# One operand group of the up-projection prepared two steps earlier, and four groups of finished outputs formed six steps later

## Chip, cores and metric

One core of a Trainium2 chip runs the whole kernel in one launch. The metric is the device time in microseconds (us), as the median over runs; before the change it is 2288.43 us over 3 runs (2288.39 to 2288.69). All matmuls are on TensorE (PE); VectorE (DVE) and ScalarE (ACT) prepare operands and drain results; SyncE (SP) issues nearly all the DMAs, in program order; GpSimd (POOL) does small copies.

## What is computed

One decoder block over 2048 positions of 1024 channels, in float32. What matters here is the chain of four large products and the norms between them:

```
h = rms_norm(x, norm1_g)
z = einsum('bsd,de->bse', h, w_in)            # in-projection
...                                           # convolutions, RG-LRU scan, gates -> y_mix
x = x + einsum('bse,ed->bsd', y_mix, w_out)   # out-projection
h = rms_norm(x, norm2_g)
u = causal_dwconv(einsum('bsd,df->bsf', h, w_up), ffn_conv_w)   # up-projection
gate, up = split(u, 2)
x = x + einsum('bsf,fd->bsd', gelu(gate) * up, w_down)          # down-projection
return rms_norm(x, final_g)
```

## The kernel before

The sequence is cut into two halves of 1024 positions (`T`), and the phases run one after the other: in-projection and mixers of half 0, out-projection of half 0, in-projection and mixers of half 1, out-projection of half 1 (the "second out-projection"), up-projection of half 0, down-projection of half 0, up-projection of half 1, down-projection of half 1 (the "last phase").

Each float32 operand of a product is split into a high part (ACT, `Copy` to a rounded form) and a low part (DVE, the difference; `split`, L196 and L197), and each product is three matmuls: high by high, high by low, low by high. The out-, up- and down-projections are done in a form of Strassen's method with seven block products in place of eight, so their operands are sums and differences of blocks.

**The sweeps.** An out- or down-projection (`sweeps`, L726 for its matmuls, L739 for its loads) makes seven sweeps over the inner dimension, one for each block product. A sweep of the out-projection has three steps (21 in all, numbered 0 to 20), one of the down-projection six (42, numbered 0 to 41). A step loads one page of weights (`wrw`) and one of the other operand (`wrf`) into four raw tiles (two steps' worth), splits both (`wh`, `wl`, `fh`, `fl`, from a pool `w` of ten pages) and runs 24 matmuls. After a sweep DVE adds the four results into the residual pages (`xr` or `x2r`, L762). At the end of every step `beside(step)` is called, which may put other work there.

**The work beside.** In the second out-projection it is `h_prep(0, k)` (L537 to L559): the preparation of operand group k of the up-projection of half 0. There are four groups; k = 0 is made in the mixers of half 1, k = 1, 2, 3 in this phase. Each loads two pages of the stored residual (`ha`, `hb`, L541, by SP), scales both (L542), forms four sums (`hc`, `hq`, L546 to L549) and splits four operands (`hhB`/`hlB` twice, `hhT`/`hlT`, `ht`): 2 DMAs, 10 DVE instructions, 4 ACT instructions. `ha` and `hb` come from a pool of two pages (tag `a`), so the loads of group k wait until group k-1 is split; the seven result pages come from the pool `act` of 28 pages.

In the last phase it is `down1_beside` (L912 on): the outputs of half 0. They wait only for the last norm, which is worked out early in the up-projection before. Four times, two pages of 512 KB are loaded (`fx`, L917), scaled (L906) and stored four steps later.

**What sets the order.** PE, SP and POOL take their instructions in the order of the program. For DVE and ACT a planner orders the instructions at compile time, by the program's order moved forward by stated priorities: splits of weights by 90 instructions (`HW`), drains of PSUM by 120 (`HP`), the adds after a sweep by 30 (`HE`). `h_prep` and `down1_beside` have none. The engines then run the order they were given. A stored page is sent some steps after it is made (`defer`, `tick`, L193).

Of the kernel before, what the change touches and what calls it, by code (L numbers as in the profile page):

```python
# [15 lines left out]
KC = D // P  # L16
# [52 lines left out]
def block_kernel(  # L69
# [52 lines left out]
    def act(name):  # L122
        return page(name, "act", 28)
# [19 lines left out]
    def flat(t):  # L143
        return t.rearrange("p a b -> p (a b)")
# [39 lines left out]
    def defer(n, dst, src):  # L184
        waiting.append([n, dst, src])
# [77 lines left out]
    def inv_rms(acc, name, parts=None):  # L263
        n = acc.shape[-1]
        terms = parts or mean_split(acc, name)
        pss = [pst(f"ms_{name}_{t}") for t in range(0, n, NB)]
        for i, x in enumerate(terms):
            for b, p in enumerate(pss):
                w, v = (ones_r, r32(x[:, blk(b)])) if i < 2 else (ones, x[:, blk(b)])
                nc.tensor.matmul(p, w, v, start=i == 0, stop=i == len(terms) - 1)  # L270
        with tc.high_priority(offset=HP):
            y = flat(tmp(f"ry_{name}"))[:, :n]
            for b, p in enumerate(pss):
                nc.scalar.activation(y[:, blk(b)], p, AF.Abs_reciprocal_sqrt, bias=eps)
                nc.vector.scalar_tensor_tensor(acc[:, blk(b)], p, EPS, y[:, blk(b)], ALU.add, ALU.mult)
            nc.vector.scalar_tensor_tensor(acc, acc, -0.5, y, ALU.mult, ALU.mult)
            nc.vector.scalar_tensor_tensor(acc, acc, 1.5, y, ALU.add, ALU.mult)
        return acc
# [258 lines left out]
    def h_prep(half, k, rs):  # L537
        a = big(f"ha{half}_{k}", 0)[:, :T]
        b = big(f"hb{half}_{k}", 0)[:, :T]
        for t, kk in ((a, k), (b, k + 4)):  # L540
            nc.sync.dma_start(t, x2_d[half][kk // 2][kk % 2])  # L541
            nc.vector.scalar_tensor_tensor(t, t, col(O_G2 + kk), rs, ALU.mult, ALU.mult)  # L542
        c = flat(tmp(f"hc{half}_{k}"))
        q = flat(tmp(f"hq{half}_{k}"))[:, :NB]
        t0, t1 = blk(0), blk(1)
        nc.vector.tensor_tensor(c[:, t0], a[:, t0], a[:, t1], ALU.subtract)  # L546
        nc.vector.scalar_tensor_tensor(c[:, t1], c[:, t0], -1.0, b[:, t1], ALU.mult, ALU.subtract)
        nc.vector.tensor_tensor(a[:, t1], b[:, t1], a[:, t1], ALU.subtract)
        nc.vector.scalar_tensor_tensor(q, c[:, t1], -1.0, b[:, t0], ALU.mult, ALU.subtract)  # L549
        out = {}  # L550
        for t, names in ((a, ("B11", "T3")), (b, ("B21", "B22")), (c, ("T1", "T2"))):
            hi, lo = act(f"hh{names[0]}{half}_{k}"), act(f"hl{names[0]}{half}_{k}")
            split(flat(hi), flat(lo), t)
            for i, n in enumerate(names):
                out[n] = (hi[:, i, :], lo[:, i, :])
        t4 = act(f"ht{half}_{k}")
        split(t4[:, 0, :], t4[:, 1, :], q)
        out["T4"] = (t4[:, 0, :], t4[:, 1, :])
        return out  # L559
# [243 lines left out]
    def store_done(dst, acc, name):  # L803
        def done(key, m, r):
            if m % 2 == 0:
                return
            mh, t = PLACE[key]
            store_pair(dst[2 * mh + m // 2], t, r, 2 if key == "21" else 4)
            add_squares(acc, t, 0 if key in ("11", "22") and m == 1 else 1, r, f"{name}{key}{m}")

        return done
# [43 lines left out]
    def h_beside(half, at):  # L855
        def beside(s):
            if s in at:
                hs[half].append(h_prep(half, len(hs[half]), rs2[half][0]))

        return beside  # L860

    def res_alloc(key, n):
# [7 lines left out]
        "o",  # L870
        x_residual(1, res_alloc),
        store_done(x2_d[1], ss2[1], "b1"),
        h_beside(0, (3, 8, 14)),
    )

    up_phase(0, hs[0], late_mean(ss2[1], "b1", rs2[1], 1))
# [28 lines left out]
    def scaled(ap, m, rs):  # L905
        nc.vector.scalar_tensor_tensor(ap, ap, col(O_GF + m), rs, ALU.mult, ALU.mult)  # L906
# [3 lines left out]
    terms = []  # L910

    def down1_beside(s):  # L912
        if s >= 4 and s % 4 == 0 and s // 4 <= KC // 2:
            i = s // 4 - 1
            for m in range(2):
                t = act(f"fx{i}_{m}")
                nc.sync.dma_start(flat(t), x3_d[i][m])  # L917
                scaled(flat(t), 2 * i + m, rs3[0])
                defer(4, yT[2 * i + m, :, 0:T], flat(t))
        if s == 6 * (NI // 2) + 1:  # L920
            finish_block(1, inv_rms(accl[1], "l1"))

    def finish_block(t, rs):
        for key in ("12", "22") if t else ("11", "21"):
            mh = PLACE[key][0]
            for p, r in enumerate(kept[key]):
                for m in range(2):
                    c = 4 * mh + 2 * p + m
                    scaled(r[:, m, :], c, rs)
                    defer(4, yT[c, :, T + t * NB : T + (t + 1) * NB], r[:, m, :])  # L930

    def down1_done(key, m, r):
# [3 lines left out]
        with tc.high_priority(offset=HP if key == "21" else 0):  # L936
# [6 lines left out]
            if key == "21" and m == 2:  # L943
                terms.extend(mean_split(accl[0], "l0"))

    sweeps(1, down_w, f_d[1], NI, "d", down_residual(1, lambda key, n: act(n)), down1_done, down1_beside, tail=4)
    finish_block(0, inv_rms(accl[0], "l0", terms))
    while waiting:
# [84 lines left out]
```

## Time and profile before

| | |
|---|---|
| median of 3 runs | 2288.43 us (2288.39 to 2288.69) |
| profiled execution, its own time | 2288.58 us |
| its span, first to last instruction | 2286.8 us |
| mean granted TensorE clock | 0.997 |
| PE busy | 2267.2 us (99%) |
| DVE busy | 1722.8 us (75%) |
| ACT busy | 1132.9 us (50%) |
| second out-projection, first matmul to first matmul of the next phase | 780.56 to 896.92 us |
| last phase, start on the chain | 2041.34 us |

The span is what the trace covers; the execution's own time is 1.8 us longer, for what lies before the first and behind the last instruction. A matmul of 512 columns shows a duration of 389 ns, but they are pipelined: in a full stretch 72 of them take 16.32 us, one each 226.7 ns. A row of the timeline gives start, duration, engine, line, operation, output and inputs, count, and in brackets how long the engine was idle before it and which instruction ended that.

### The profile page before, as it was taken

What the parts mean: (1) busy time and instruction counts of PE and PEld (TensorE: products, weight loads), DVE (VectorE), ACT (ScalarE), POOL (GpSimd) and SP (SyncE); (2) the same over time, 40 slices, a digit from 0 to 9 for tenths busy, and PEclk for the clock granted to TensorE, in tenths of its full rate; (3) what the DMA queues carried; (4) which work ended last, traced back from release to release, by engine and by line L of the source; (5) the groups of instructions that cost most, each with busy time, mean ns of one, the idle gap of its engine ahead of it and who ended that gap; (6) DMA issues with size and microseconds to landing.
All of it is one profiled execution on the core that took longest, in us unless ns stands there. A gap on an engine that the chain in (4) does not pass through costs nothing.

```text
span 2286.8 us, 26184 instructions
## 1 busy us (share of the span) xinstructions
PE 2267.2 (99%) x9984; PEld 1874.0 (82%) x9984; DVE 1722.8 (75%) x1909; ACT 1132.9 (50%) x1242; POOL 154.2 (7%) x232
## 2 busy tenths in 40 slices
PE   9999999999999999999999999999999999999997
PEld 7888888888888878888888888888888888888885
DVE  7665668857667798888888887587888888876556
ACT  6564635554547255544444444354544444443343
POOL 0011000011000000111111100000100000000000
PEclk9999999999999999999999999999999999999999
DMA  6454248777655576223232357676223232359764
GB/s 260 122 134 118 70 161 280 259 203 219 167 149 144 180 268 216 87 97 116 92 117 91 118 187 268 217 242 210 71 97 115 92 115 92 116 184 318 262 189 174
DMA packets 145728, 378.30 MB, mean 165 GB/s; under 512 B 13953, under 2 KB 17153, under 8 KB 145025
## 3 DMA queue, kind: packets, MB, share of 16 engines
q1 hardware_dynamic: 135808, 357.74, 45.3%
q0 software_dynamic: 9792, 18.88, 5.2%
q8 instruction: 78, 1.28, 0.2%
q14 instruction: 50, 0.40, 0.1%
HBM read 289.53 MB, written 124.78 MB: 181 GB/s over the span
## 4 chain that ended last, share of the span: by engine, by line
PE 98%; DVE 1%; issue 0%; DMA 0%; ACT 0%; SPq 0%; DVEq 0%
PE zin_b L236 27%; PE zx L606 23%; PE zc L606 11%; PE dx L726 11%; PE dy L726 9%; PE za L606 6%; PE ox L726 6%; PE oy L726 4%; PE zi_b L236 1%; PE zr_b L236 1%; DVE x2r L906 0%; DMA x<-in_xT 0%; DVE wl_d L197 0%; DVE fl_o L197 0%; PE ms_a L270 0%
## 5 line engine op out<-in xcount | busy, mean ns | idle before, releaser
L236 PE MATMUL zin_b<-xh,wh_in 128*128 128x512 f32 x896 | 276.8, 390 | 2.7 <-ACT xh L409 2.7
L236 PE MATMUL zin_b<-xl,wh_in 128*128 128x512 f32 x896 | 276.6, 390 | 0.3 <-DVE xl L410 0.3
L236 PE MATMUL zin_b<-xh,wl_in 128*128 128x512 f32 x896 | 276.3, 390 | 0.0
L236 PEld LDWEIGHTS zin_b<-xh,wh_in 128*128 128x128 f32 x896 | 168.5, 188 | 38.3 <-ACT xh L409 3.3
L236 PEld LDWEIGHTS zin_b<-xl,wh_in 128*128 128x128 f32 x896 | 168.2, 188 | 36.4 <-DVE xl L410 1.8
L236 PEld LDWEIGHTS zin_b<-xh,wl_in 128*128 128x128 f32 x896 | 168.4, 188 | 35.0
L197 DVE TENSOR_TENSOR fl_d<-wrf_d,fh_d 128x1024 fp32r<-128x1024 f32 x84 | 102.8, 1224 | 121.8 <-ACT fh_d L196 119.4
L196 ACT ACTIVATE fh_d<-wrf_d 128x1024 fp32r<-128x1024 f32 x84 | 89.1, 1061 | 209.1 <-PE dy L726 86.4
L197 DVE TENSOR_TENSOR wla_up<-wra_up,wha_up 128x1024 fp32r<-128x1024 f32 x48 | 58.8, 1226 | 140.5 <-ACT wha_up L196 140.5
L726 PE MATMUL dx<-fl_d,wh_d 128*128 128x512 f32 x384 | 149.5, 389 | 0.8 <-DVE fl_d L197 0.8
L726 PE MATMUL dx<-fh_d,wh_d 128*128 128x512 f32 x384 | 149.4, 389 | 0.0
L726 PE MATMUL dx<-fh_d,wl_d 128*128 128x512 f32 x384 | 149.4, 389 | 0.0
L606 PE MATMUL zc<-hhB,whd_up 128*128 128x512 f32 x384 | 126.0, 389 | 0.0
L299 DVE SCALAR_TENSOR_TENSOR cu<-un,prm,cu 128x1024 f32<-128x1024 f32 x96 | 122.6, 1277 | 4.4 <-ACT cu L295 4.3
L299 DVE SCALAR_TENSOR_TENSOR cg<-ug,prm,cg 128x1024 f32<-128x1024 f32 x96 | 122.8, 1280 | 0.4
L196 ACT ACTIVATE wh_in<-wr_in 128x1024 fp32r<-128x1024 f32 (+1 forms) x62 | 59.8, 972 | 122.2 <-PE zin_b L236 93.4
L617 ACT ACTIVATE ug<-zx 128x512 f32<-128x512 f32 x96 | 57.6, 600 | 125.9 <-PE zx L606 125.9
L606 PE MATMUL zx<-ht,whc_up 128*128 128x512 f32 x384 | 118.2, 389 | 0.0
L197 DVE TENSOR_TENSOR wl_d<-wrw_d,wh_d 128x1024 fp32r<-128x1024 f32 x84 | 102.4, 1220 | 12.8 <-ACT wh_d L196 11.5
L726 PE MATMUL dy<-fh_d,wh_d 128*128 128x512 f32 x288 | 112.0, 389 | 0.0
L726 PE MATMUL dy<-fl_d,wh_d 128*128 128x512 f32 x288 | 112.0, 389 | 0.0
L726 PE MATMUL dy<-fh_d,wl_d 128*128 128x512 f32 x288 | 112.0, 389 | 0.0
(261 smaller groups left out, 5552.5 us busy)
## 6 DMA issues: line engine op xcount, KB each, us to landing
wr_in<-in_w_in SPq DMA_DIRECT2D x54, 512.0 KB, 6.7
wra_up<-in_w_up SPq DMA_DIRECT2D x48, 512.0 KB, 4.7
wrb_up<-in_w_up SPq DMA_DIRECT2D x48, 512.0 KB, 5.3
f_d_T<-cg SPq DMA_DIRECT2D x96, 256.0 KB, 2.5
wrw_d<-sd_d_S SPq DMA_DIRECT2D x48, 512.0 KB, 4.5
wrf_d<-f_d_T SPq DMA_DIRECT2D x48, 512.0 KB, 3.9
f_d_B<-cu SPq DMA_DIRECT2D x72, 256.0 KB, 2.4
wrw_d<-in_w_down SPq DMA_DIRECT2D x36, 512.0 KB, 4.7
```

Source lines behind the costliest of these rows:

```text
L196: nc.scalar.activation(r32(hi), src, AF.Copy)
L197: nc.vector.tensor_tensor(r32(lo), src, hi, ALU.subtract)
L236: nc.tensor.matmul(ps[t], r32(a), r32(b[:, blk(t)]), start=(first and i == 0), stop=(last and i == 2))
L299: nc.vector.scalar_tensor_tensor(dst, src[:, k : k + T], col(o_w + k), dst, ALU.mult, ALU.add)
L606: nc.tensor.matmul(ps, r32(p[:, s]), r32(self.hs[k][x][o]), start=f and i == 0, stop=l and i == 2, skip_group_check=True,)
L617: nc.scalar.activation(dst, self.x, AF.Copy)
L726: nc.tensor.matmul(ps[m], r32(p), r32(x[:, k, :]), start=first and i == 0 and n == 0, stop=(last or not on_x) and i == ni - 1 and n == 2, ...
```

## The change

`h_beside(0, ...)` is called for steps 1, 8 and 14 of the second out-projection in place of 3, 8 and 14: `h_prep(0, 1)` stands at the end of step 1, in front of step 2's loads. In the last phase the four groups of outputs of half 0 are loaded and scaled in steps 10, 14, 18 and 22 in place of 4, 8, 12 and 16; the groups and their order stay the same, and each is stored four steps later as before.

```diff
         "o",
         x_residual(1, res_alloc),
         store_done(x2_d[1], ss2[1], "b1"),
-        h_beside(0, (3, 8, 14)),
+        h_beside(0, (1, 8, 14)),
     )
...
     def down1_beside(s):
-        if s >= 4 and s % 4 == 0 and s // 4 <= KC // 2:
-            i = s // 4 - 1
+        if 10 <= s <= 22 and s % 4 == 2:
+            i = s // 4 - 2
             for m in range(2):
                 t = act(f"fx{i}_{m}")
                 nc.sync.dma_start(flat(t), x3_d[i][m])
```

## Rows read from the trace of the kernel before

**Rows 1.** The page: busy time, share and count of each engine, and the shares of the chain of work that ended last.

```profile
PE 2267.2 (99%) x9984; PEld 1874.0 (82%) x9984; DVE 1722.8 (75%) x1909; ACT 1132.9 (50%) x1242; POOL 154.2 (7%) x232
...
PE 98%; DVE 1%; issue 0%; DMA 0%; ACT 0%; SPq 0%; DVEq 0%
```

**Rows 2.** The waits of PE over the whole span: who waited for whom, us in total, how often, the longest.

```profile
PE oy L726 <- DVE fl_o L197: 1.5, 2, 0.9
...
PE dx L726 <- DVE fl_d L197: 0.8, 1, 0.8
```

**Rows 3.** Busy time of each engine in the first and second sweep of the second out-projection: the window, its length, then busy us and count for PE, PEld, DVE, ACT and POOL, the granted clock, the DMA share and GB/s.

```profile
780.56:796.88 16.32, 16.32 (x73) 13.51 (x72) 13.33 (x15) 4.86 (x6) 0.00 (x0) 1.00 0.55 194
796.88:815.32 18.44, 16.91 (x74) 13.36 (x72) 17.91 (x20) 9.37 (x10) 0.00 (x0) 1.00 0.61 186
```

**Rows 4.** Timeline of PE in that second sweep: the first two matmuls of its second step, and the first two of its third.

```profile
802.32 0.39 PE L726 MATMUL oy<-fh_o,wh_o 128*128 128x512 f32 x1
803.61 0.50 PE L726 MATMUL oy<-fl_o,wh_o 128*128 128x512 f32 x1 [0.90 <-DVE fl_o L197]
...
808.96 0.39 PE L726 MATMUL oy<-fh_o,wh_o 128*128 128x512 f32 x1
809.97 0.50 PE L726 MATMUL oy<-fl_o,wh_o 128*128 128x512 f32 x1 [0.63 <-DVE fl_o L197]
```

**Rows 5.** Timeline of DVE in the same sweep: instructions of `h_prep(0, 1)` (`ha`, `hlB`, `ht`) among the splits of the steps (`wl_o`, `fl_o`).

```profile
797.01 1.28 DVE L542 SCALAR_TENSOR_TENSOR ha<-ha,prm,ss_b 128x1024 f32<-128x1024 f32 x1
...
800.60 1.22 DVE L197 TENSOR_TENSOR wl_o<-wrw_o,wh_o 128x1024 fp32r<-128x1024 f32 x1
...
802.34 1.22 DVE L197 TENSOR_TENSOR fl_o<-wrf_o,fh_o 128x1024 fp32r<-128x1024 f32 x1
...
807.56 1.22 DVE L197 TENSOR_TENSOR hlB<-hb,hhB 128x1024 fp32r<-128x1024 f32 x1
808.70 1.22 DVE L197 TENSOR_TENSOR fl_o<-wrf_o,fh_o 128x1024 fp32r<-128x1024 f32 x1
...
813.24 0.69 DVE L197 TENSOR_TENSOR ht<-hq,ht 128x512 fp32r<-128x512 f32 x1
```

**Rows 6.** Timeline of ACT: the split of step 2's weights, and later two splits, one of `h_prep(0, 1)` and one of a step's weights.

```profile
780.31 1.06 ACT L196 ACTIVATE wh_o<-wrw_o 128x1024 fp32r<-128x1024 f32 x1 [5.91 <-PE zin_b L236]
...
804.19 1.06 ACT L196 ACTIVATE hhB<-ha 128x1024 fp32r<-128x1024 f32 x1 [6.28 <-DVE ha L548]
805.16 1.04 ACT L196 ACTIVATE wh_o<-wrw_o 128x1024 fp32r<-128x1024 f32 x1
```

**Rows 7.** Timeline of SP's queue: the residual page of step 1, the second operand of step 2, the residual page of step 2, the weights of step 3, the first load of `h_prep(0, 1)`, and the weights of step 5.

```profile
756.33 0.40 SPq L527 DMA_DIRECT2D xr<-in_xT  x1
...
757.38 0.37 SPq L739 DMA_DIRECT2D wrf_o<-y_d_B  x1
770.78 0.38 SPq L527 DMA_DIRECT2D xr<-in_xT  x1
771.25 0.42 SPq L739 DMA_DIRECT2D wrw_o<-so_d_S  x1
...
773.59 0.57 SPq L541 DMA_DIRECT2D ha<-x_d  x1
...
790.96 0.32 SPq L739 DMA_DIRECT2D wrw_o<-so_d_S  x1
```

**Rows 8.** Timeline of DVE before that: the last reads of `ha` and `hb` of group 0, the instructions behind its idle stretches, and the second operand's low part of steps 2 (788.58) and 3 (792.56).

```profile
758.94 1.23 DVE L197 TENSOR_TENSOR hlB<-ha,hhB 128x1024 fp32r<-128x1024 f32 x1 [0.53 <-ACT hhB L196]
760.09 1.22 DVE L197 TENSOR_TENSOR hlB<-hb,hhB 128x1024 fp32r<-128x1024 f32 x1
...
769.66 1.29 DVE L379 TENSOR_TENSOR pr<-zin_b,ss_a 128x512 f32<-128x512 f32 x2 [4.28 <-PE zin_b L236]
...
772.00 1.22 DVE L387 TENSOR_TENSOR pr<-pr,cc 128x1024 f32<-128x1024 f32 x1
780.54 1.29 DVE L379 TENSOR_TENSOR sb<-zin_b,ss_a 128x512 f32<-128x512 f32 x2 [7.32 <-PE zin_b L236]
...
788.58 1.22 DVE L197 TENSOR_TENSOR fl_o<-wrf_o,fh_o 128x1024 fp32r<-128x1024 f32 x1
...
792.56 1.23 DVE L197 TENSOR_TENSOR fl_o<-wrf_o,fh_o 128x1024 fp32r<-128x1024 f32 x1 [1.62 <-ACT fh_o L196]
```

**Rows 9.** The waits of SP's queue over the whole span, the row of the residual loads.

```profile
SPq L527 <- PE zin_b L236: 12.9, 1, 12.9
```

**Rows 10.** DMA issues by line: count, KB each, median us from issue to landing.

```profile
wrw_o<-in_w_out SPq DMA_DIRECT2D x18, 512.0 KB, 5.7
...
ha<-x_d SPq DMA_DIRECT2D x8, 512.0 KB, 5.5
hb<-x_d SPq DMA_DIRECT2D x8, 512.0 KB, 6.5
```

**Rows 11.** The windows of the first, second and fourth sweep of the last phase, columns as in the third group.

```profile
2041.34:2073.98 32.64, 32.64 (x145) 27.03 (x145) 24.61 (x24) 12.57 (x13) 0.00 (x0) 1.00 0.82 290
2073.98:2106.62 32.64, 32.64 (x145) 27.03 (x145) 20.79 (x20) 12.35 (x13) 0.00 (x0) 1.00 0.97 336
...
2139.26:2171.90 32.64, 32.64 (x145) 27.03 (x145) 16.90 (x17) 13.12 (x15) 0.00 (x0) 1.00 0.70 230
```

**Rows 12.** Timeline of DVE in the last phase: one scaling of outputs of half 0 (two instructions).

```profile
2103.22 2.48 DVE L906 SCALAR_TENSOR_TENSOR fx<-fx,prm,ss_c 128x1024 f32<-128x1024 f32 x2
```

## The prediction

> **What bounds the kernel now.** I read the shares first: PE is busy 99% of the span and the chain that ended last is PE for 98% of it [rows 1]. So a change can win only where PE stands still, and lose only where it makes PE stand still. Next the waits of PE: two of them, 1.5 us together, are in a `y` sweep of an out-projection and wait for `fl_o`, the low part that DVE makes; one of 0.8 us is in a `dx` sweep [rows 2]. Then the windows by sweep: the first sweep of the second out-projection takes 16.32 us, which is 72 matmuls of 226.7 ns back to back; the second takes 18.44 us, 2.12 us more, with DVE busy 17.91 of them [rows 3]. The timeline of PE places it: in step 4 the second matmul starts 1.29 us after the first in place of 0.23 us, in step 5 it starts 1.01 us after [rows 4]. That is 1.06 and 0.78 us, together 1.84; the other 0.28 us is the pace of the few matmuls that follow a stop. The order of DVE says why: the `h_prep(0, 1)` instructions stand between the splits of steps 4 and 5 from 797.01 to 813.93 us, and `fl_o` of step 4 starts only at 802.34, that of step 5 at 808.70, behind `hlB` [rows 5].
>
> **Part 1, the operand group two steps sooner.** It moves 2 loads on SP, 10 instructions on DVE and 4 on ACT; none is added or removed, and POOL's queue has none of it. On DVE: two scalings of 1.28 us, four sums of 512 columns of 0.69 us each (the form of `ht`), three low parts of 1.22 us and `ht` of 0.69 us [rows 5]: 2.56 + 2.76 + 3.66 + 0.69 = 9.7 us. On ACT: three high parts of 1.06 us [rows 6] and half a one, about 3.7 us.
>
> *When the loads can go.* They stand behind step 1's residual load, issued at 756.33 [rows 7]. `ha` needs the page whose last reader, `hlB` of group 0, ends at 760.17, `hb` the one that ends at 761.31 [rows 8]; 5.5 and 6.5 us to landing [rows 10] give about 766 and 768 us. Before they were issued at 773.59 [rows 7].
>
> *What is queued behind them on SP.* Step 2's loads, the second issued at 757.38 [rows 7], move to about 762; with 5.7 us to landing [rows 10] they are there at 768 and are first read at 780.31 [rows 6]: 12 us of cover, cost nothing. Then step 2's residual load, which already waits 12.9 us for a page that PE's last in-projection frees [rows 9]. The seven result pages of the group now take pages ahead of it. That product frees two pages for each six matmuls (6 x 0.2267 = 1.36 us), so seven pages are 3.5 x 1.36 = 4.8 us: the residual load goes from 770.78 to about 775.5, step 3's weights from 771.25 [rows 7] to about 776, landed by 782. Step 3's last split, `fl_o`, came at 792.56 [rows 8], and its weights go first, by my estimate some 5 us sooner: about 5 us of cover, cost nothing. Without that cover each us would be a us of PE.
>
> *Where DVE does it.* Between 755 and 797 us DVE has two idle stretches: 4.28 us up to 769.66, and 7.32 us from 773.22 to 780.54, waiting for PE [rows 8]. Together 11.6 us for 9.7 us of work, and ACT is idle for 5.91 us up to 780.31 [rows 6], for 3.7 us of work. If the scalings fall before 769.66 or right behind 773.2, the group is done between about 780 and 783 us. I take the first, as the loads' estimated landing (766 and 768) lies in the first stretch.
>
> *What it leaves.* 9.7 us go from a window in which DVE was busy 17.91 of 18.44 us [rows 3]; `wl_o` and `fl_o` of steps 4 and 5 then stand right behind the adds of sweep 0, some 2 to 4 us sooner than needed. Both stalls go: -2.12 us. Next late would be the adds at the end of this sweep, but PE's waits hold none for those [rows 2]. The preparation of groups 2 and 3 keeps its steps and has none either. Bounds for part 1: -2.12 us (nothing else there stands still) and, at the far end, +5.7 us (rival D).
>
> **Part 2, the outputs formed later.** 8 loads, 8 scalings and 8 stores move by 6 steps, one sweep (32.64 us). PE is busy for all 32.64 us of the sweeps shown [rows 11], and the waits of PE hold one wait in `dx`, 0.8 us [rows 2], which lies behind the last sweep's residual work: nothing is there to win. Relief of the DMAs (share 0.97 in the second sweep, [rows 11]) is worth nothing, as nobody on the chain waits for them. What could be lost: a pair of scalings is 2.48 us on DVE [rows 12]. Steps 18 and 22 lie in the fourth sweep, where DVE is busy 16.90 us [rows 11]; two pairs make it 21.9, less than the 24.61 us that the first sweep carries without a stop [rows 11]. On SP the loads and stores are as many as before, ahead of the same kind of loads. Bounds: 0, and +2.2 us if a pair meets the four adds at a sweep's end (2.5 + 4 x 0.69 = 5.2 us, less about 3 us that a split runs ahead of its step). I take 0, by the row of the first sweep.
>
> **Sum.** -2.12 + 0 us against the profiled execution: 2288.58 - 2.12 = 2286.46 us. The median lies 0.15 us below that execution, so **2286.3 us**.
>
> **Rivals.**
>
> *B, half the gain.* The scalings come only behind 773.2 us: 773.2 + 9.7 + 0.5 us for the hop to ACT and back = 783.4, so 2.9 us spill behind 780.54, where the mixers' last work and step 2's splits stand. `fl_o` of step 2 ends at 789.80 [rows 8] and PE would ask for it at 780.56 + 2 x 5.44 + 0.23 = 791.67: 1.87 us ahead. So PE loses 1.0 us there and wins 1.1 net: 2287.3 us. For it: a load may take more than the median. Against: ACT and DVE are nearly free up to 780.
>
> *C, no change.* The planner does not take the group sooner than before, or puts something else ahead of the splits of steps 4 and 5, so that the move doesn't do what it says: 2288.4 us. For it: with `ha` issued at 773.59 [rows 7] and likely landed by 780, DVE scaled it only at 797.01 [rows 5] and left 1.62 us idle before 792.56 [rows 8]: the planner's order is not the earliest possible. Against: in the new place nothing of higher priority is ready in 7.32 us.
>
> *D, slower.* A new wait in place of the old: the planner puts the group behind `sb` at 780.54, among the splits of steps 2 and 3, and the engines hold to that order. That they do shows already: ACT stood idle for 6.28 us until DVE's `ha` was ready, while the weights of step 5, issued at 790.96 [rows 7] and so landed by about 797, were split only behind it, at 805.16 [rows 6]. With all 9.7 us ahead of `fl_o` of step 2, which has 1.87 us to spare, PE stops for 7.8 us; less the 2.12 won later, +5.7: 2294.1 us. With half, 4.85 - 1.87 = 3.0, less 2.12, +0.9: 2289.3 us. It decides from the point where more than 1.87 + 2.12 = 4.0 us of the group lies between 780.54 and 788.58. Against it: the idle stretch of 7.32 us lies just before, and the data are there by my estimate 5 us ahead of it.
>
> The Trainium skill (Perfetto Trace Analysis, Tensor Engine Instruction) says that ACT and DVE are strict FIFO, with no reordering as TensorE has; this speaks against any early, low-priority work that is not ready in time. The trace agrees, by the 6.28 us [rows 6]. Were the engines free to pass a waiting instruction, the group could be put early at no risk and the sum would be 2286.3 us in any order; by the rule D stands, up to 2294.1 us.
>
> **How the numbers follow.** My forecast A (2286.0 to 2286.7) gets 0.70: the idle stretches are in the trace and hold the work. B 0.10, C 0.08, D 0.11 (0.04 of it near its far end), and 0.01 for more than A, if the `dx` wait of 0.8 us goes too (2285.5). The range 2285.7 to 2288.7 holds A, B and C, 0.88, and takes in part 2's upper bound (2286.3 + 2.2 = 2288.5); D lies above it. About 0.2%, 4.6 us, is what a measurement of this kernel can tell from no change: faster by more means below 2283.9, which no case reaches (0.01); slower by more means above 2293.0, D's far end and what I have not seen (0.05); between them 0.94.
>
> **What would show it.** Right: in the new trace `ha` and `hb` of the group are issued at 760 to 762 us and scaled before 781; the waits of PE for `fl_o` in the second out-projection are gone, its second sweep takes 16.3 us, and the first matmul of the up-projection starts at about 894.8 in place of 896.92 us; the last phase is as long as before, with PE waiting for nothing in its first six sweeps. Wrong: PE waits for `fl_o` or `wl_o` in steps 2 or 3 (B, D), `wl_o` of step 4 still starts near 800 us (C), or a wait shows in the fourth sweep of the last phase (part 2).

## The result and the profile after

The changed kernel takes 2294.75 us in the median of 7 runs (2294.3 to 2296.76), the kernel before 2288.43 (2288.25 to 2288.7, 7 runs). The ratio is 1.003, with a 95% interval of 1.002 to 1.004: **slower by 6.3 us, 0.28%**. The forecast was 2286.3 us, the far end of rival D 2294.1. The profiled execution of the changed kernel took 2294.75 us, its span is 2293.0 us and its mean granted clock 0.995, against 0.997 before.

The waits of PE over the whole span (who waited for whom, us in total, how often, the longest):

```profile
PE oy L726 <- DVE fl_o L197: 4.0, 1, 4.0
...
PE oy L726 <- ACT fh_o L196: 1.1, 1, 1.1
...
PE ox L726 <- DVE fl_o L197: 0.9, 1, 0.9
...
PE dx L726 <- DVE fl_d L197: 0.8, 1, 0.8
```

The two waits of [rows 2] in the `y` sweep are gone, as forecast, and three new ones of 6.0 us together have come in the out-projection. The `dx` wait is as it was.

Timeline of SP's queue, the part that answers to [rows 7]:

```profile
759.64 0.32 SPq L541 DMA_DIRECT2D ha<-x_d  x1
760.78 0.32 SPq L541 DMA_DIRECT2D hb<-x_d  x1
...
774.32 0.38 SPq L527 DMA_DIRECT2D xr<-in_xT  x1
774.75 0.46 SPq L739 DMA_DIRECT2D wrw_o<-so_d_S  x1
```

The DMA view of the stretch from 755 to 780 us (count, KB, median us from issue to landing):

```profile
ha<-x_d SPq DMA_DIRECT2D x1, 512.0 KB, 3.3
hb<-x_d SPq DMA_DIRECT2D x1, 512.0 KB, 4.8
```

So SP does what was forecast. The loads go at 759.64 and 760.78 and are there at about 762.9 and 765.6 us. The next residual load has moved to 774.32 and step 3's weights to 774.75, where 775.5 and 776 were forecast.

Timeline of DVE (start, duration, instruction; in brackets the idle time before it and its releaser), which answers to [rows 8] and [rows 5]:

```profile
769.11 1.29 DVE L379 TENSOR_TENSOR pr<-zin_b,ss_a 128x512 f32<-128x512 f32 x2 [4.29 <-PE zin_b L236]
...
779.99 1.29 DVE L379 TENSOR_TENSOR sb<-zin_b,ss_a 128x512 f32<-128x512 f32 x2 [7.32 <-PE zin_b L236]
...
784.97 1.28 DVE L542 SCALAR_TENSOR_TENSOR ha<-ha,prm,ss_b 128x1024 f32<-128x1024 f32 x1
...
787.37 1.27 DVE L542 SCALAR_TENSOR_TENSOR hb<-hb,prm,ss_b 128x1024 f32<-128x1024 f32 x1
...
789.17 1.21 DVE L197 TENSOR_TENSOR wl_o<-wrw_o,wh_o 128x1024 fp32r<-128x1024 f32 x1
790.31 0.68 DVE L546 TENSOR_TENSOR hc<-ha 128x512 f32<-128x512 f32 x1
790.91 1.21 DVE L197 TENSOR_TENSOR fl_o<-wrf_o,fh_o 128x1024 fp32r<-128x1024 f32 x1
...
799.07 0.69 DVE L197 TENSOR_TENSOR ht<-hq,ht 128x512 fp32r<-128x512 f32 x1
799.67 1.28 DVE L762 TENSOR_TENSOR xr<-xr,ox 128x512 f32<-128x512 f32 x2
800.86 1.22 DVE L197 TENSOR_TENSOR wl_o<-wrw_o,wh_o 128x1024 fp32r<-128x1024 f32 x1
802.00 1.22 DVE L197 TENSOR_TENSOR fl_o<-wrf_o,fh_o 128x1024 fp32r<-128x1024 f32 x1
```

This is where the forecast breaks. Both idle stretches, 4.29 and 7.32 us, are as long as in [rows 8], though `ha` had landed 17 us before `sb` began. `ha` is scaled at 784.97, behind the last mixer's drain. `ha`, `hb` and the first `hc` stand ahead of `fl_o` of step 2; the other seven instructions stand between that one and `wl_o` of step 3.

Timeline of ACT, which answers to [rows 6]:

```profile
793.36 1.06 ACT L196 ACTIVATE hhB<-ha 128x1024 fp32r<-128x1024 f32 x1 [6.87 <-DVE ha L548]
...
796.75 1.04 ACT L196 ACTIVATE wh_o<-wrw_o 128x1024 fp32r<-128x1024 f32 x1
797.69 1.04 ACT L196 ACTIVATE fh_o<-wrf_o 128x1024 fp32r<-128x1024 f32 x1
```

ACT idles 6.87 us for DVE's `ha` of the group, though step 3's weights, issued at 774.75, had landed 5.4 us later, at about 780.2; step 3's own two splits stand behind the group's four and end at 797.79 and 798.73.

Timeline of PE at the three waits, and the first matmul of the up-projection:

```profile
790.90 0.39 PE L726 MATMUL ox<-fh_o,wh_o 128*128 128x512 f32 x1
792.18 0.50 PE L726 MATMUL ox<-fl_o,wh_o 128*128 128x512 f32 x1 [0.89 <-DVE fl_o L197]
...
797.30 0.39 PE L726 MATMUL ox<-fh_o,wl_o 128*128 128x512 f32 x1
798.78 0.49 PE L726 MATMUL oy<-fh_o,wh_o 128*128 128x512 f32 x1 [1.09 <-ACT fh_o L196]
803.27 0.80 PE L726 MATMUL oy<-fl_o,wh_o 128*128 128x512 f32 x1 [4.00 <-DVE fl_o L197]
803.87 0.63 PE L726 MATMUL oy<-fh_o,wl_o 128*128 128x512 f32 x1
...
807.81 0.39 PE L726 MATMUL oy<-fh_o,wh_o 128*128 128x512 f32 x1
...
903.02 0.39 PE L606 MATMUL zx<-hhB,wha_up 128*128 128x512 f32 x1
```

Windows over that stretch (length, busy us and count for PE, PEld, DVE, ACT and POOL, then the granted clock, DMA share and GB/s), and below them the second and fourth sweep of the last phase:

```profile
801.00:804.00 3.00, 0.73 (x2) 0.63 (x3) 3.00 (x3) 0.00 (x0) 0.00 (x0) 0.50 0.25 78
804.00:807.00 3.00, 3.00 (x9) 2.32 (x8) 1.94 (x3) 1.06 (x1) 0.00 (x0) 0.50 0.85 255
2080.10:2112.80 32.70, 32.70 (x146) 27.09 (x145) 19.91 (x21) 12.13 (x13) 0.00 (x0) 1.00 0.74 247
2145.40:2178.10 32.70, 32.70 (x146) 27.09 (x145) 21.10 (x22) 13.39 (x15) 0.00 (x0) 1.00 0.82 262
```

In the wait of 4.00 us the granted clock falls to 0.50 of full speed, the lower of the two levels (1.2 GHz), and stays there for some 4 us of running. The matmuls then start 0.43 us apart instead of 0.227.

**Where the time went.** The stage runs from 780.02 us, its first matmul, to 903.02, 123.0 us; seven sweeps of 16.32 are 114.24, so 8.76 us are lost, against 2.12 before. Starts that lie further apart than 0.23 us give 1.05 us (step 2), 1.25 (`fh_o` of step 3) and 4.26 (`fl_o` of step 3). From 803.27 to 807.81 there are 11 intervals in 4.54 us, where 2.49 would do: 2.05 us for the clock. Together 8.6 of the 8.76. The net loss is 6.6 us; the stage began 0.54 us earlier in this execution, which leaves 6.1 of the 6.2 us that the span grew by.

The last phase costs nothing. PE is busy for every microsecond of both sweeps, as in [rows 11]. The DMA share of the second fell from 0.97 to 0.74, and DVE in the fourth rose from 16.90 to 21.1 us.

### The profile page after: what moved, and what is told of

It is laid out like the page before. It is cut to its first block, busy times and chain, and to the rows that moved or that the text cites. A ratio compares the mean times of both kernels' runs of the same rounds, so it can differ in the third digit from the quotient of the medians.

```text
span 2293.0 us, 26179 instructions
## 1 busy us (share of the span) xinstructions
PE 2269.8 (99%) x9984; PEld 1876.2 (82%) x9984; DVE 1721.9 (75%) x1909; ACT 1132.2 (49%) x1242; POOL 155.6 (7%) x232
## 4 chain that ended last, share of the span: by engine, by line
PE 97%; DVE 2%; issue 0%; ACT 0%; DMA 0%; SPq 0%; DVEq 0%; ACTq 0%
PE zin_b L236 27%; PE zx L606 23%; PE zc L606 11%; PE dx L726 11%; PE dy L726 9%; PE za L606 6%; PE ox L726 5%; PE oy L726 4%; PE zi_b L236 1%; PE zr_b L236 1%; DVE x2r L906 0%; DMA x<-in_xT 0%; DVE sv L299 0%; DVE wl_d L197 0%; DVE fl_o L197 0%
```

## The experiments

The question was why ten instructions with their data ready did not run in 11.6 us of idle time, and what the slow matmuls add. The theory O (order): DVE and ACT keep to the order that the planner gave them, and it put the group behind the last mixer and among the splits of steps 2 and 3. Its rivals: the data were not there in time; the earlier loads or their pages themselves cost the time; part 2 costs it. A second theory, C (clock): the fall of the clock after the waits has a price of its own. A third, Q: what was written ahead of the group decides where the planner puts it. The first four kernels ran beside a kernel before at 2288.55 us (29 runs), the last three beside one at 2288.65 us (25 runs).

**Part 1 alone.**

```diff
-        h_beside(0, (3, 8, 14)),
+        h_beside(0, (1, 8, 14)),
```

> Only the first part: the operand group at step 1, the outputs of the last phase at steps 4, 8, 12 and 16 as before. Theory O (order: the planner put the group's ten VectorE and four ScalarE instructions among the splits of steps 2 and 3, and engines that hold to their order make TensorE wait): 2294.7 us, within 2294.0 to 2297, with the same three waits in steps 2 and 3 as the changed kernel. Theory P (the second part costs or gives something): the difference to 2294.7 us is what it is worth, up to 2.2 us.

It took 2295.58 us (2295.13 to 2295.91, 6 runs), ratio 1.003 [1.0019, 1.0041]. PE has the same three waits of 0.9, 1.1 and 4.0 us. The whole loss is part 1's. It took 0.8 us more than the changed kernel; its trace shows 12 matmuls at half clock in place of 9, which is 0.6 us of that.

**Part 2 alone.**

```diff
-        if s >= 4 and s % 4 == 0 and s // 4 <= KC // 2:
-            i = s // 4 - 1
+        if 10 <= s <= 22 and s % 4 == 2:
+            i = s // 4 - 2
```

> Only the second part: the outputs of the last phase at steps 10, 14, 18 and 22, the operand group at step 3 as before. Theory O: 2288.4 us within 0.3, and no wait of TensorE in the first six sweeps of the last phase. Theory P: another time than 2288.4, up to 2290.6 us.

2288.31 us (2287.75 to 2288.88, 10 runs), ratio 0.9999 [0.999, 1.0008], with the 1.5 us of waits in `oy` as before. Part 2 is worth nothing, as its step said.

**The same move, with the last mixer's end written behind the group.** Loads and their order on SP stay as in part 1; the drain, convolution and sums of the last mixer step of half 1 stand behind the group in the program.

```diff
-        sbt = flat(act(f"sb{half}_{s}"))
-        evac(sbt, ps, rs)
...
+        def rest():
+            sbt = flat(act(f"sb{half}_{s}"))
+            evac(sbt, ps, rs)
...
+        return rest if half == 1 and s == NSC - 1 else rest()
...
                 hs[half].append(h_prep(half, len(hs[half]), rs2[half][0]))
+                if half == 0 and tails:
+                    tails.pop()()
...
-        h_beside(0, (3, 8, 14)),
+        h_beside(0, (1, 8, 14)),
```

> The first part alone, with the same loads at the same place in SyncE's queue; but the last mixer's drain, convolution and sums are written in the program behind the group, so that the planner can put the group into VectorE's idle stretches at 765 to 770 and 773 to 780 us. Theory O (the place in the order costs, not the moved loads, pages or work): the waits in steps 2 to 5 are gone and the time is 2286.3 us, 2285.7 to 2287.3. Theory R (the moved loads, the pages that the group takes or its work so early cost the time): no faster than 2288.4, and about 2294 if all of it stays.

2286.55 us (2285.79 to 2287.31, 11 runs), ratio 0.999 [0.9981, 0.9999]. Its DVE timeline:

```profile
764.87 1.28 DVE L555 SCALAR_TENSOR_TENSOR ha<-ha,prm,ss_b 128x1024 f32<-128x1024 f32 x1
...
766.79 1.28 DVE L555 SCALAR_TENSOR_TENSOR hb<-hb,prm,ss_b 128x1024 f32<-128x1024 f32 x1
...
778.54 0.68 DVE L198 TENSOR_TENSOR ht<-hq,ht 128x512 fp32r<-128x512 f32 x1
780.12 1.29 DVE L380 TENSOR_TENSOR sb<-zin_b,ss_a 128x512 f32<-128x512 f32 x2 [0.89 <-PE zin_b L237]
```

And its chain of work (start, length, what, count):

```profile
780.31 16.32 PE ox L739 x72
...
894.55 2.72 PE zx L619 x12
```

All ten instructions lie between 764.87 and 779.2, `sb` is on time, and seven sweeps take 114.24 us with no wait. This is the forecast's mechanism and nearly its time (2286.3). It rules out late data, and shows that the idle stretches hold the group. What was missing is the order. It is also the fastest version run: 2.0 us under the kernel before, with an interval that only just excludes no change.

**Only the loads early.** The two loads are issued at the end of step 1, and the group's 10 instructions on DVE and 4 on ACT are held behind step 3's `fl_o`. `h_load` is the two loads taken out of `h_prep`, and `last_split` the low part that was written last.

```diff
...
+            if half == 0 and s == 1:
+                early.append(h_load(0, 1))
             if s in at:
-                hs[half].append(h_prep(half, len(hs[half]), rs2[half][0]))
+                with tc.issue_after(last_split[0].ins) if early else ExitStack():
+                    hs[half].append(h_prep(half, len(hs[half]), rs2[half][0], early.pop() if early else None))
```

> The first part alone, with the group's loads at step 1, but its instructions written at step 3 and queued on VectorE behind the low part of step 3's second operand. Theory O: TensorE no longer waits in steps 2 and 3; the group then stands about where it stood before, though behind the splits of step 4: 2286.3 to 2288.4 us. Theory R (the loads and pages at step 1 cost): about 2294.

2287.21 us (2286.62 to 2288.03, 10 runs), ratio 0.9994 [0.9985, 1.0004]: no slower than the kernel before, and the gain of 1.3 us is not clear of no change. The one wait of PE that is left in the out-projection, then `fl_o` of step 3 and `ha` of the group on DVE:

```profile
PE oy L732 <- DVE fl_o L198: 0.6, 1, 0.6
...
795.14 1.22 DVE L198 TENSOR_TENSOR fl_o<-wrf_o,fh_o 128x1024 fp32r<-128x1024 f32 x1
...
798.07 1.28 DVE L548 SCALAR_TENSOR_TENSOR ha<-ha,prm,ss_b 128x1024 f32<-128x1024 f32 x1
```

The up-projection begins at 895.42 on the chain of work. So loads ahead of step 2's on SP, and two pages held longer, cost nothing. Only the place of the DVE and ACT work does.

**The wait filled.** The changed kernel with 14 more matmuls behind the first of step 3, into a PSUM tile that is free; their results are discarded.

```diff
+                        if name == "o" and half == 1 and s == 1 and i == 0 and k == 0 and m == 0 and n == 0:
+                            for _ in range(14):
+                                nc.tensor.matmul(
+                                    ps[3], r32(p), r32(x[:, k, :]), start=True, stop=True, skip_group_check=True
+                                )
```

> The changed kernel with 14 extra matmuls of 512 columns put into TensorE's queue behind the first matmul of step 3, on operands that are there; they write a bank that the step's own first matmul of that bank clears. They fill about 3.2 of the 4.3 us in which TensorE waits for the low part of step 3's second operand; the wait's end stays where it is. Theory C (the clock's fall to 1.2 GHz behind that wait costs time of its own, 9 matmuls at 0.43 us in place of 0.23): the granted clock stays at full speed and about 2.0 us are won, 2292.7 us, 2292.2 to 2293.5. Rival (what was lost is the wait alone, or TensorE catches up later): 2294.7 us or more.

2293.14 us (2292.68 to 2293.94, 10 runs), ratio 1.002 [1.0011, 1.0029]. PE's timeline:

```profile
798.87 3.38 PE L736 MATMUL oy<-fh_o,wh_o 128*128 128x512 f32 x14
803.02 0.50 PE L726 MATMUL oy<-fl_o,wh_o 128*128 128x512 f32 x1 [0.77 <-DVE fl_o L197]
```

Its window, for the second one of the changed kernel above:

```profile
804.00:807.00 3.00, 3.00 (x14) 2.46 (x14) 1.84 (x3) 1.06 (x1) 0.00 (x0) 1.00 0.83 238
```

The rest of the sweep on the chain of work, here and then in the changed kernel:

```profile
803.02 16.41 PE oy L726 x71
...
803.27 18.30 PE oy L726 x71
```

The work still waits for `fl_o`, and restarts at 803.02 in place of 803.27 only because the whole stage began 0.25 us earlier in this execution. But it restarts at full clock: 14 matmuls in a window that held 9, and 16.41 us in place of 18.30 for the 71 matmuls. So the fall of the clock costs 1.9 us of its own. In the medians it is 1.6 us, or 1.8 when each kernel is set against the kernel before that ran beside it.

**One other load moved.** Part 1, but the residual load of step 1 is written behind the group instead of ahead of it.

```diff
+                late = name == "o" and half == 1 and step == 1
+                if not late:
+                    for key, p in fetch.get((s, i2), ()):
+                        res.setdefault(key, []).append(residual(key, p))
...
+                if late:
+                    for key, p in fetch.get((s, i2), ()):
+                        res.setdefault(key, []).append(residual(key, p))
```

> The first part alone, and step 1's residual load (xr) written behind the group in place of ahead of it. Theory Q (the planner took the group's loads for late, because in its plan the residual page of step 1, whose load stands ahead of them on SyncE, had to wait for the mixer's last pages, though on the chip it was free): the two scalings now run at about 765 to 770 us, in the idle stretch; the other eight instructions still stand behind the mixer's last sums, as their pages come behind the mixer's in the program, and ahead of step 2's splits: one wait in step 2 of about 5 us (0 in steps 3 to 5), so 2291.3 us, or 2293.5 if the clock falls behind it. Theory R (the loads themselves land late): the scalings stay behind 780 us and the time is that of the changed kernel, 2294.7.

2294.36 us (2293.07 to 2295.36, 10 runs), ratio 1.0024 [1.0015, 1.0033]. Its DVE timeline:

```profile
765.54 1.28 DVE L542 SCALAR_TENSOR_TENSOR ha<-ha,prm,ss_b 128x1024 f32<-128x1024 f32 x1
766.74 1.28 DVE L542 SCALAR_TENSOR_TENSOR hb<-hb,prm,ss_b 128x1024 f32<-128x1024 f32 x1
...
787.12 0.68 DVE L546 TENSOR_TENSOR hc<-ha 128x512 f32<-128x512 f32 x1
...
794.75 1.22 DVE L197 TENSOR_TENSOR wl_o<-wrw_o,wh_o 128x1024 fp32r<-128x1024 f32 x1
```

And its ACT timeline:

```profile
789.64 1.06 ACT L196 ACTIVATE hhB<-ha 128x1024 fp32r<-128x1024 f32 x1 [14.97 <-DVE ha L548]
```

Moving one load that the group does not use puts the two scalings into the idle stretch; so their place followed from what was written ahead of them. The other eight still stand behind two of the mixer's three sums, now all ahead of step 2's `wl_o`. Step 2's own loads now go at 774.67 and 775.22, behind the residual load, but have landed by 783, long before their splits on ACT at 793.03 and 793.97; so it is the order again that they wait for. PE waits 3.2 us for `fh_o` and 1.6 for `fl_o`, 4.8 us, where about 5 were expected; 23 matmuls behind the second wait take 8.10 us on the chain in place of 5.21, so the clock costs 2.9 us here. 4.8 + 2.9 - 2.1 = 5.6, and 5.7 was measured. The time itself missed: it is 0.9 us above the 2293.5 that was expected with a fall of the clock, whose price was put too low, and close to the 2294.7 of late loads. What decides between the two is where the scalings stand, not the time.

**One step sooner instead of two.**

```diff
-        h_beside(0, (3, 8, 14)),
+        h_beside(0, (2, 8, 14)),
```

> The first part alone with the group at step 2 in place of 1 (before: 3). Theory O (what stands between the splits sets the waits): step 2's splits go ahead of the group, so no wait in step 2; the group's first half stands ahead of step 3's low part and the second half ahead of step 4's: waits of about 1.8 and 3.0 us, together 4.8 against 2.1 before: 2291.1 us, 2289.5 to 2293 (more if the clock falls). A rival by which earlier is worse in proportion: half way between 2288.5 and 2295, 2291.7 us, with waits in step 2.

2290.96 us (2289.18 to 2291.93, 10 runs), ratio 1.0009 [0.9999, 1.0018], which is not quite clear of no change. The time came out near the expectation, but not by its terms: the waits, 1.8 and 3.0 us expected in steps 3 and 4, are 0.50 and 2.34, and the clock adds the rest. No wait stands in step 2, where the rival by which earlier is worse in proportion had put them; its time, 2291.7 us, is within the runs. PE's timeline:

```profile
805.77 0.50 PE L726 MATMUL oy<-fl_o,wh_o 128*128 128x512 f32 x1 [2.34 <-DVE fl_o L197]
...
807.39 0.63 PE L726 MATMUL oy<-fl_o,wh_o 128*128 128x512 f32 x1
```

And a window of it:

```profile
808.00:810.00 2.00, 2.00 (x7) 1.52 (x6) 0.94 (x1) 1.03 (x1) 0.00 (x0) 0.50 0.97 322
```

The 47 matmuls from 805.77 on take 12.59 us on the chain in place of 10.65: 1.9 us.

## Why the prediction was wrong

**The step that failed is "Where DVE does it".** It chose the idle stretches because the data would be there. They were, some 3 us sooner than estimated (762.9 and 765.6 against 766 and 768), and the stretches were long enough, as the kernel with the mixer's end written later shows. But readiness decides nothing on an engine whose order is fixed at compile time, and no row of before showed the order that the planner would choose. The text had the sign of it under rival C and gave it too little weight (C and D together had 0.19): an `ha` that was scaled only at 797.01. It was said to have landed by 780; in the trace it took 9.7 us and landed at 783.3, still 13.7 us before it was used.

The Trainium skill (Perfetto Trace Analysis, Tensor Engine Instruction) says that ACT and DVE are strict FIFO. The traces agree: ACT stood still for 6.87 us, and for 14.97 us in one experiment, with splits queued behind the waiting one whose weights had landed by about 780 us in both.

**Rival D is what happened, with its terms off.** It put all 9.7 us ahead of `fl_o` of step 2, a stop of 7.8 us. Only `ha`, `hb` and `hc`, 3.0 us of DVE's time, stand there, and the stop is 1.05 us. The rest falls on step 3, whose `fl_o` starts 9.99 us later against `sb` than in [rows 8] (802.00 - 779.99 against 792.56 - 780.54). There the four adds at the end of sweep 0 come ahead of it too, 2.4 us. By D's own point (over 4.0 us ahead of `fl_o` of step 2) the change would not have lost: that point looked at one step, and the delay carries over to the next.

**One term was missing, the clock:** 2.05 us. The 1.25 us that PE waits for `fh_o` of step 3, because ACT's splits stand behind the group's, is not a further term. It is the first part of the stop that `fl_o` sets: that one had 3.3 us to spare before (it ended at 793.79 [rows 8], and PE asked for it at 796.88 + 0.23), it came 9.99 us later, and DVE has no idle time between its start on `hlB` at 794.46 and `fl_o`. 9.99 - 3.3 = 6.7 us is what the three stops come to, 1.05 + 1.25 + 4.26 = 6.56. D had 7.8 - 2.1 = 5.7; measured is 1.05 + 1.25 + 4.26 + 2.05 + 0.15 - 2.12 = 6.6, so D was near partly by chance: its stops were too long by 1.2 us and the clock made up for it.

**What held.** The issue times of the loads and of the residual load behind them, the cover of step 2's and step 3's loads (the waits for `fh_o` and `fl_o` end with ACT and DVE, no DMA), the 2.12 us that are to be had (2.0 between the medians of 2288.55 and 2286.55), and part 2 at nothing, with DVE at 21.1 us in the fourth sweep where 21.9 was worked out.

**What stays open** is why the planner orders so. That the order of writing decides the place is shown by two kernels. That its own times let the group wait for pages that are handed out in program order, first to the residual load and then to the mixer's last tiles, is argued only. A priority for the group alone was not tried on the chip.

## What to carry to other kernels

An earlier line in the program is not an earlier place in an engine's queue: before an idle stretch is counted as cover, find out what the order will put into it, and write the work that should fill it ahead of the work that it should pass. Low-priority work that lands among the splits of an engine that holds to its order delays not only the next split: here `fl_o` of step 2 by 2.9 us and that of step 3 by 10.0. A long stop of TensorE can have a second price behind it, matmuls at half clock: here single waits of 2.34 and 4.00 us did, and those of 0.9 us and less in the out-projection did not; where between them it begins was not measured.

## What the runs showed of the hardware

After waits of 1.09 and 4.00 us the granted clock was 0.50 and 9 to 12 matmuls ran 0.43 us apart (9 in the changed kernel, 12 in part 1 alone with the same waits); after 3.18 and 1.60 us it was 12 (the residual load written behind). After a wait of 2.34 us the clock fell as well, some 1.4 us after PE had started again, for 8 matmuls. The waits of 0.90 and 0.63 us of [rows 4] left it at full speed, and so did the wait that was filled with matmuls but for 0.77 us.

The Trainium skill (TensorE: Matmul & The Clock Gate, What's actually happening) says that the throttled level is the default and activity releases it, and that the number of slow matmuls varies between runs of one kernel. The windows at 0.50 and 1.00 agree, and the 9 and 12 fit the second: the two kernels are the same up to the last phase.

The prediction had no term for the clock, though the kernel before has such a stretch too. At its very start PE waits 2.21 us, until 7.51 us, and from about 8 to 11 us it runs at 0.50:

```profile
10.00:11.00 1.00, 1.00 (x4) 0.79 (x3) 0.42 (x1) 0.32 (x2) 0.00 (x0) 0.50 1.08 320
```
